# A hybrid decoder layer on one core: score maxima kept by group and reduced once per unit, reciprocals taken for two units at once

## The chip, the cores and the metric

The kernel runs on one core of a Trainium2 chip. The metric is the device time of one execution in microseconds, as the median of several runs. Times inside an execution come from one profiled execution, whose own time is given beside its span (from its first instruction to its last).

The core has engines that run side by side, each with its own queue of instructions in order: PE (matrix products, into PSUM), DVE (vector operations), ACT (activation functions, copies with a scale), POOL (a second, slower vector engine) and SP (which here issues transfers). They wait for each other through semaphores.

## The reference

The layer has forgetting attention with 8 heads of width 64 beside a gated short convolution, then an output projection and a convolutional feed-forward part, over 2048 positions of width 1024, all in float32. The change touches the attention alone:

```python
for i in range(s // BLOCK_Q):                    # 16 blocks of 128 queries
    q0, q1 = i * BLOCK_Q, (i + 1) * BLOCK_Q
    logits = einsum('bqhd,bkhd->bhqk', q[:, q0:q1], k[:, :q1]) * scale
    logits = logits + fcum[:, :, q0:q1, None] - fcum[:, :, None, :q1]
    logits = where(causal, logits, -inf)
    p = softmax(logits, axis=-1)
    outs.append(einsum('bhqk,bkhd->bqhd', p, v[:, :q1]))
```

A query block i sees (i + 1) blocks of 128 keys, and its softmax needs the row's maximum over all of them.

## The kernel before

The program has three stretches: projections and convolution (0 to 597 us of the span), attention (597 to 925 us), output projection and feed-forward part (925 us to the end).

In attention a **unit** is a pair of query blocks of one head, 15 - u and u for u = 0 to 7, so that each unit has 17 key blocks. There are 8 x 8 = 64 units, numbered n = 8h + u in what follows. The loop over s starts one unit per step, and each step runs five generators in turn, a piece of each per round: `weights` of unit s-1, `scores` of unit s, `divide_early` of unit s-4, `turn` of unit s-2 and `values` of unit s-4. Nearly all instructions are held in the order in which the program issues them, so this interleaving is each engine's queue.

What a unit goes through:

- `scores`: each query block's keys are cut into chunks of 512 columns, together five chunks per unit, taken in the order block 15-u, block u, block 15-u, and so on. PE makes a chunk's scores in a PSUM tile `ps` (lines 1053, 1054, and 1056 for the causal mask; four such tiles). DVE then adds the forget term `nf`, writes the scores to `s_t` and takes the running maximum into a column of `mx` (line 1077). This is one instruction with a second one behind it that reads the accumulator out. The operation of a block's later chunks starts its maximum from the column of the chunk before, through a pointer, so the last column holds the block's maximum. For u = 0 to 3 the first block has four chunks and the second one, so three chunks of the same block come one right after the other; for u = 4 to 7 the blocks alternate.
- `weights`: ACT scales the two maxima into a bias `nb` (line 1091) and runs two exponentials over `s_t` (line 1094), which also add up the row sums `l`.
- `turn`: POOL splits the far part of the weights into two halves (lines 1105, 1106), which a transfer transposes. For the near part PE transposes nine blocks into three PSUM tiles `pt` (line 1114), ACT evicts each to `near` (line 1116), and DVE subtracts for the low half (line 1121). DVE also takes the reciprocal of `l` here (line 1124).
- `values`: PE multiplies the weights with the values into `po` (lines 1150 to 1152). DVE divides, that is multiplies by the reciprocal (line 1165), and PE's next products into `po` wait for that.

Every second head, around u = 0 and u = 4, `store` transposes finished output and copies it out through ACT (`tm`, line 1184). In some steps ACT also takes sums over the output weights (`junk`, line 916).

Of the kernel before, what the change touches and what calls it, by code (L numbers as in the profile page):

```python
# [9 lines left out]
F32 = mybir.dt.float32  # L10
# [5 lines left out]
ALU = mybir.AluOpType  # L16
AX = mybir.AxisListType
# [3 lines left out]
P = 128  # L21
# [7 lines left out]
NT = S // P  # L29
# [17 lines left out]
def kernel(  # L47
# [20 lines left out]
    V, A, G, T = nc.vector, nc.scalar, nc.gpsimd, nc.tensor  # L68
# [72 lines left out]
    K = tc.keep_in_program_order  # L141
# [872 lines left out]
    with ExitStack() as ph:  # L1014
        cs = ph.enter_context(tc.tile_pool(name="cs", bufs=6))
# [28 lines left out]
        def product(g):  # L1044

            if len(products) > g:
                return
            while len(products) < min(g + GROUP, len(chunks)):
                h, u, _, i, c0, cw, last = chunks[len(products)]
                kh, qs, kl, nf = heads[h]  # L1050
                qt = qs[:, i * P : (i + 1) * P]
                ps = ps_s.tile([P, 512], F32, tag="s", name="ps")
                K(T.matmul(ps[:, 0:cw], lhsT=qt, rhs=kh[:, c0 : c0 + cw], start=True, stop=False))  # L1053
                K(T.matmul(ps[:, 0:cw], lhsT=qt, rhs=kl[:, c0 : c0 + cw], start=False, stop=not last))  # L1054
                if last:
                    K(T.matmul(ps[:, cw - P : cw], lhsT=ident_b, rhs=maskb, start=False, stop=True))  # L1056
                products.append(ps)

        taken[0] = 0

        def scores(un):

            nf = heads[un["h"]][3]
            un["s"] = s_t = cs.tile([P, WU], F32, tag="s", name="s_t", bufs=3)
            mx = cs.tile([P, 4, 4], F32, tag="mx", name="mx")[:, 0:2, :]
            un["l"] = cs.tile([P, 2], F32, tag="l", name="l", bufs=12)
            un["parts"] = [(NT - 1 - un["u"], NT - un["u"], 0), (un["u"], un["u"] + 1, NT - un["u"])]
            ends = [0, 0]
            while taken[0] < len(chunks) and chunks[taken[0]][:2] == (un["h"], un["u"]):
                _, _, p, i, c0, cw, last = chunks[taken[0]]  # L1070
                o0 = p * (NT - un["u"]) * P
                product(taken[0] + LEAD)
                ps = products[taken[0]]
                products[taken[0]] = None
                taken[0] += 1
                g = c0 // 512
                K(V.tensor_tensor_reduce(  # L1077
                    out=s_t[:, o0 + c0 : o0 + c0 + cw], in0=ps[:, 0:cw], in1=nf[:, c0 : c0 + cw], scale=1.0,
                    scalar=-3.0e38 if g == 0 else mx[:, p, g - 1 : g],
                    op0=ALU.add, op1=ALU.max, accum_out=mx[:, p, g : g + 1],  # L1080
                ))
                if last:
                    ends[p] = 4 * p + g
                yield
            un["mx"] = mx.rearrange("p a g -> p (a g)")[:, ends[0] : ends[1] + 1 : ends[1] - ends[0]]

        def weights(un):

# [9 lines left out]
        def turn(un):  # L1098

            s_t = un["s"]  # L1100
            near = cp.tile([P, 2, WB, P], F16, tag="near", name="near", bufs=3)
            far = cp.tile([P, 2, NT + 1 - WB, P], F16, tag="far", name="far", bufs=3)
            un["t"] = near, far
            wide = un["wide"]
            K(G.tensor_scalar(wide[:, 0, :], s_t[:, WB * P : WU], 1.0, 0.0, op0=ALU.mult, op1=ALU.add))
            K(G.tensor_tensor(wide[:, 1, :], s_t[:, WB * P : WU], wide[:, 0, :], op=ALU.subtract))  # L1106
            nc.sync.dma_start_transpose(far.rearrange("p a b n -> p (a b) n"), wide.rearrange("p a n -> p (a n)"))
            late = []

            def blocks(b0):  # L1110
                nb = min(4, WB - b0)
                pt = ps_x.tile([P, 512], F32, tag="x", name="pt")
                for b in range(nb):
                    K(T.transpose(pt[:, b * P : (b + 1) * P], s_t[:, (b0 + b) * P : (b0 + b + 1) * P], ident))  # L1114
                th, tl = [near[:, a, b0 : b0 + nb, :].rearrange("p b n -> p (b n)") for a in range(2)]
                K(A.activation(th, pt[:, 0 : nb * P], AF.Copy))  # L1116
                late.append((tl, pt[:, 0 : nb * P], th))

            def rest():
                tl, pt, th = late.pop(0)  # L1120
                K(V.tensor_tensor(tl, pt, th, op=ALU.subtract))  # L1121

            yield
            K(V.reciprocal(un["l"], un["l"]))
            yield
            blocks(0)
            yield
            blocks(4)
            yield
            blocks(8)  # L1130
            rest()
            yield
            rest()
            yield
            rest()
# [52 lines left out]
        units = []  # L1188
# [4 lines left out]
        for s in range(H * nu + 8):  # L1193
            h, u = divmod(s, nu)
# [13 lines left out]
            for back, stage in ((1, weights), (0, scores), (4, divide_early), (2, turn), (4, values)):  # L1208
                if 0 <= s - back < H * nu:
                    run.append(stage(units[s - back]))  # L1210
# [39 lines left out]
    with ExitStack() as ph:  # L1250
# [104 lines left out]
        def norm2_late(Q):  # L1355
# [19 lines left out]
            if Q % 2 == 0:  # L1375
                for k in range(4):
                    for n, name in enumerate(("b11", "b21")):
                        affine = turn(Q, 4 * n + k)
                        if later:
                            later.pop()()  # L1380
                        yield
                        h = affine()
                        hi, lo = pair(name, k)
                        high(h, hi)
                        later.append(lambda h=h, hi=hi, lo=lo: low(h, hi, lo))
                        yield
                later.pop()()
                yield
                return
# [38 lines left out]
            for k in range(4):  # L1428
                first = turn(Q, k)
                go_on()  # L1430
                yield
                b1 = first()
                go_on()
                yield
                second = turn(Q, 4 + k)
                go_on()
                yield
                b2 = second()
                go_on()
                running.append(sums(k, b1, b2))  # L1440
                yield
# [393 lines left out]
```

## Time and profile before

| | us |
|---|---|
| median of 3 runs | 2356.49 |
| lowest and highest run | 2356.17, 2357.16 |
| profiled execution, its own time | 2353.64 |
| its span | 2351.9 |
| mean granted clock of PE | 0.997 |
| PE busy over the span | 2270.3 |
| DVE busy over the span | 1742.2 |
| ACT busy over the span | 1164.3 |
| POOL busy over the span | 339.2 |

In a row of the profile, "L1077 DVE ... s_t<-ps,nf,mx" is line, engine, operation, and the tiles written and read. The group rows give shape, count, busy time in us, mean ns of one, and idle time of the engine ahead of them. Instructions overlap a little: the next may start before the one ahead has ended, so a pace is read from start to start. In rows by time the first number is the start, the second the duration, and square brackets hold the idle time ahead and what ended it.

### The profile page before, as it was taken

To read this page: it belongs to the slowest core of one execution; us is meant where nothing else is said; L and a number is where in the kernel's file an instruction comes from. 1 tells how busy PE (TensorE), PEld (TensorE's weight loads), DVE (VectorE), ACT (ScalarE), POOL (GpSimd) and SP (SyncE) were. 2 spreads that over 40 slices of the span, in tenths; PEclk is the share of its full clock that TensorE was granted. 3 is DMA by queue.
4 is the path that set the end of the run, shared out by engine and by line. 5 is a ranking of instruction groups with operands and counts; after the bars stand their busy time and mean duration, and the time that the engine had idled before them with its cause. 6 is when DMAs were issued, how large, how long until landed. Compare 5 with 4: busy or idle time off the path is not lost.

```text
span 2351.9 us, 38578 instructions
## 1 busy us (share of the span) xinstructions
PE 2270.3 (97%) x14208; PEld 1354.2 (58%) x14208; DVE 1742.2 (74%) x3414; ACT 1164.3 (50%) x1992; POOL 339.2 (14%) x282
## 2 busy tenths in 40 slices
PE   5899999999899998999999999999999999999999
PEld 5765554444577776444444444588764444446887
DVE  6768895773899998556899999966966565656556
ACT  5745453321688887343555565565522223224333
POOL 0211111111688874001000000000000000000000
PEclk9999999999999999999999999999999999999999
DMA  9346599973799986534456656577764454445766
GB/s 287 136 151 183 157 263 291 301 238 90 150 195 191 215 170 138 190 108 163 155 192 224 217 199 210 213 264 236 219 224 147 153 161 143 156 158 190 234 210 220
DMA packets 452646, 455.25 MB, mean 194 GB/s; under 512 B 191248, under 2 KB 301160, under 8 KB 451432
## 3 DMA queue, kind: packets, MB, share of 16 engines
q1 hardware_dynamic: 445336, 435.94, 62.4%
q10 hardware_dynamic: 4752, 8.46, 1.0%
q0 software_dynamic: 2368, 8.39, 0.9%
q8 instruction: 111, 1.82, 0.3%
q14 instruction: 79, 0.65, 0.1%
HBM read 284.84 MB, written 134.28 MB: 178 GB/s over the span
## 4 chain that ended last, share of the span: by engine, by line
PE 80%; DVE 11%; ACT 5%; issue 2%; DMA 1%; SPq 1%; POOL 0%; DVEq 0%; ACTq 0%
PE acc L1611 28%; PE acc L1788 16%; PE acc L145 13%; PE pr L145 11%; PE pv L145 2%; DVE s_t L1077 2%; PE pt L1114 2%; DVE near L1121 2%; PE ps L1053 1%; ACT s_t L1094 1%; PE ps L1054 1%; DVE t L1446 1%; PE po L1150 1%; ACT near L1116 1%; PE po L1152 1%
## 5 line engine op out<-in xcount | busy, mean ns | idle before, releaser
L1611 PEld LDWEIGHTS <-pair 128*128 128x128 f16 x3696 | 361.5, 98 | 439.7 <-issue 5.0
L1611 PE MATMUL acc<-t,pair 128*128 128x512 f16 x2112 | 477.4, 379 | 1.9 <-DVE t L1446 1.9
L1611 PE MATMUL acc<-b,pair 128*128 128x512 f16 x1584 | 363.4, 379 | 0.0
L1624 DVE SCALAR_TENSOR_TENSOR w<-w,fcw,w 128x1024 f32<-128x1024 f32 x176 | 226.1, 1285 | 79.4 <-ACT w L1619 73.2
L1535 DVE TENSOR_TENSOR lo<-raw,hi 128x1024 fp32r<-128x1024 f32 x154 | 187.4, 1223 | 115.8 <-ACT hi L1534 106.6
L1534 ACT ACTIVATE hi<-raw 128x1024 fp32r<-128x1024 f32 x154 | 161.1, 1057 | 172.6 <-PE acc L1788 117.9
L1788 PE MATMUL acc<-lo,hi 128*128 128x512 f32 x616 | 240.3, 390 | 2.9 <-DVE lo L1535 2.7
L1788 PE MATMUL acc<-hi 128*128 128x512 f32 x616 | 241.9, 393 | 0.0
L1788 PE MATMUL acc<-hi,lo 128*128 128x512 f32 x616 | 240.1, 390 | 0.0
L145 PEld LDWEIGHTS <-h 128*128 128x128 f16 x1344 | 130.3, 98 | 97.5 <-DVE h L358 5.4
L1619 ACT ACTIVATE w<-w,fcw 128x1024 f32<-128x1024 f32 x88 | 100.6, 1144 | 160.7 <-DVE w L1446 160.7
L145 PE MATMUL acc<-wp,mp 128*128 128x512 f16 x756 | 168.8, 382 | 2.8 <-ACT mp L954 1.4
L1094 ACT ACTIVATE s_t<-s_t,nb,cst 128x2048 f32<-128x2048 f32 (+15 forms) x128 | 164.7, 1288 | 5.8
L1106 POOL TENSOR_TENSOR wide<-s_t,wide 128x1024 f16<-128x1024 f32 x64 | 136.8, 2137 | 5.3
L1077 DVE CUSTOM_DVE_ANT_0 s_t<-ps,nf,mx 128x512 f32<-128x512 f32 (+1 forms) x192 | 119.4, 643 | 17.1 <-PE ps L1056 9.2
L1788 PEld LDWEIGHTS acc<-lo,hi 128*128 128x128 f32 x616 | 115.7, 188 | 28.1 <-DVE lo L1535 4.7
L1788 PEld LDWEIGHTS acc<-hi 128*128 128x128 f32 x616 | 115.7, 188 | 24.3 <-ACT hi L1534 0.4
L1788 PEld LDWEIGHTS acc<-hi,lo 128*128 128x128 f32 x616 | 115.6, 188 | 24.3
L145 PE MATMUL pr<-h,wh 128*128 128x512 f16 x576 | 126.5, 379 | 0.0
L145 PEld LDWEIGHTS <-mp 128*128 128x128 f16 x756 | 74.0, 98 | 90.1 <-issue 3.6
L145 PE MATMUL pr<-h,wl 128*128 128x512 f16 x576 | 125.8, 379 | 0.0
L1053 PE MATMUL ps<-kh,qs 128*128 128x512 f16 (+1 forms) x320 | 110.2, 348 | 13.2 <-DVE mx L1077 11.3
(369 smaller groups left out, 4091.1 us busy)
## 6 DMA issues: line engine op xcount, KB each, us to landing
up_sc<-pair SPq DMA_DIRECT2D x132, 256.0 KB, 2.7
pair<-up_sc SPq DMA_DIRECT2D x132, 256.0 KB, 3.0
wx<-in_w_up_dram SPq DMA_DIRECT2D x88, 256.0 KB, 3.7
raw<-in_w_up_dram SPq DMA_DIRECT2D x44, 512.0 KB, 3.7
y_t<-t SPq DMA_DIRECT2D x88, 256.0 KB, 2.7
raw<-y_t SPq DMA_DIRECT2D x88, 256.0 KB, 3.4
raw<-w_sc SPq DMA_DIRECT2D x88, 256.0 KB, 4.7
y_b<-y SPq DMA_DIRECT2D x66, 256.0 KB, 2.0
```

The costliest lines, as they stand in the source:

```text
L145: ins = T.matmul(acc, lhsT=a, rhs=b, start=st, stop=sp)
L1053: K(T.matmul(ps[:, 0:cw], lhsT=qt, rhs=kh[:, c0 : c0 + cw], start=True, stop=False))
L1077: K(V.tensor_tensor_reduce(out=s_t[:, o0 + c0 : o0 + c0 + cw], in0=ps[:, 0:cw], in1=nf[:, c0 : c0 + cw], scale=1.0, scalar=-3.0e38 if g == ...
L1094: K(A.activation(cols, cols, AF.Exp, bias=nb[:, p : p + 1], scale=qk[:, 4:5], accum_out=un["l"][:, p : p + 1]))
L1106: K(G.tensor_tensor(wide[:, 1, :], s_t[:, WB * P : WU], wide[:, 0, :], op=ALU.subtract))
L1114: K(T.transpose(pt[:, b * P : (b + 1) * P], s_t[:, (b0 + b) * P : (b0 + b + 1) * P], ident))
L1534: K(A.activation(hi, raw, AF.Copy))
L1535: K(V.tensor_tensor(lo, raw, hi.bitcast(F32), op=ALU.subtract))
L1611: K(T.matmul(acc, lhsT=a, rhs=b, start=st, stop=sp, skip_group_check=True))
L1619: K(A.activation(y, u[:, 0:1024], AF.Copy, scale=fcw[:, ct : ct + 1]))
L1624: K(V.scalar_tensor_tensor(y, u[:, m : m + 1024], fcw[:, m * 44 + ct : m * 44 + ct + 1], y, op0=ALU.mult, op1=ALU.add))
L1788: K(T.matmul(acc[t], lhsT=a[:, c], rhs=b, start=st, stop=sp, skip_group_check=True))
```

## The change

Three edits, all in the attention stretch:

- Each chunk's maximum is taken by itself, from the constant -3.0e38, into column g of its block in a tile `top` of 2 x 4 columns. There are eight such tiles, one for each u, which stay for all heads; POOL sets them to -3.0e38 once, before attention. A column that a unit doesn't use keeps that value.
- After a unit's five chunks one DVE `tensor_reduce` takes the maximum over the four columns of both blocks into a small `mx`, from which ACT makes `nb`. The generator issues it one round later than the last chunk.
- The row sums of two units share one tile of four columns, and one reciprocal of the four is taken in `turn` of the odd unit.

```diff
+        tops = [cs.tile([P, 2, 4], F32, name=f"top{u}", bufs=1) for u in range(NT // 2)]
+        for top in tops:
+            G.memset(top, -3.0e38)
...
-            mx = cs.tile([P, 4, 4], F32, tag="mx", name="mx")[:, 0:2, :]
-            un["l"] = cs.tile([P, 2], F32, tag="l", name="l", bufs=12)
+            mx = tops[un["u"]]
+            if un["u"] % 2 == 0:
+                un["ll"] = cs.tile([P, 4], F32, tag="l", name="l", bufs=6)
+            else:
+                un["ll"] = units[-2]["ll"]
+            un["l"] = un["ll"][:, 2 * (un["u"] % 2) : 2 * (un["u"] % 2) + 2]
...
-                    scalar=-3.0e38 if g == 0 else mx[:, p, g - 1 : g],
+                    scalar=-3.0e38,
...
-                if last:
-                    ends[p] = 4 * p + g
                 yield
-            un["mx"] = mx.rearrange("p a g -> p (a g)")[:, ends[0] : ends[1] + 1 : ends[1] - ends[0]]
+            un["mx"] = cs.tile([P, 2], F32, tag="mx", name="mx")
+            K(V.tensor_reduce(un["mx"], mx, axis=AX.X, op=ALU.max))
...
-            K(V.reciprocal(un["l"], un["l"]))
+            if un["u"] % 2:
+                K(V.reciprocal(un["ll"], un["ll"]))
```

The queues of PE, ACT and SP keep their order; POOL's gets the eight memsets. DVE's changes in each unit. Here is DVE's queue before for unit 24 (u = 0), from its first score operation to the subtractions of unit 22 that are issued in the same step. ISA is the score operation or, with `mx 128x1`, its read-out; the brackets name the engines and transfers it waits for.

```order
L1077 ISA s_t,mx<-ps,nf 128x512 [waits DMAHW4_49,PE_49,Pool_49]
L1077 ISA mx 128x1
L1077 ISA s_t,mx<-ps,nf 128x128 [waits PE_49]
L1077 ISA mx 128x1
L1124 RECIPROCAL l<-l 128x2
L1077 ISA s_t,mx<-ps,nf,mx 128x512 [waits DVE_49,PE_49]
L1077 ISA mx 128x1
...
L1121 TENSOR_TENSOR near<-pt,near 128x512 [waits Activation_49] x2
L1165 TENSOR_TENSOR at<-po,l 128x2x64 [waits PE_49]
L1121 TENSOR_TENSOR near<-pt,near 128x128 [waits Activation_49]
```

(The fourth and fifth score operations, left out, read like the third.) And DVE's queue with the change at the same place, where `top_6769` is the persistent tile of u = 0:

```order
L1083 ISA s_t,top_6769<-ps,nf 128x512 [waits DMAHW4_49,PE_49,Pool_49]
L1083 ISA top_6769 128x1
L1083 ISA s_t,top_6769<-ps,nf 128x128 [waits PE_49]
L1083 ISA top_6769 128x1
L1083 ISA s_t,top_6769<-ps,nf 128x512 [waits PE_49]
L1083 ISA top_6769 128x1
...
L1126 TENSOR_TENSOR near<-pt,near 128x512 [waits Activation_49]
L1090 TENSOR_REDUCE mx<-top_6769 128x2 [waits DVE_49]
L1126 TENSOR_TENSOR near<-pt,near 128x512 [waits Activation_49]
L1171 TENSOR_TENSOR at<-po,l 128x2x64 [waits PE_49]
L1126 TENSOR_TENSOR near<-pt,near 128x128 [waits Activation_49]
```

(Here too the fourth and the fifth are left out.) The waits of score operations on DVE itself are gone, the reciprocal has left this even unit, and a reduction stands between the first and the second subtraction.

The second place is unit 29 (u = 5), DVE's queue from its last score operation to the first of unit 30, before:

```order
L1077 ISA s_t,mx<-ps,nf,mx 128x384 [waits DVE_49,PE_49]
L1077 ISA mx 128x1
L1121 TENSOR_TENSOR near<-pt,near 128x512 [waits Activation_49]
L1165 TENSOR_TENSOR at<-po,l 128x2x64 [waits PE_49]
L1121 TENSOR_TENSOR near<-pt,near 128x512 [waits Activation_49]
L1121 TENSOR_TENSOR near<-pt,near 128x128 [waits Activation_49]
L1077 ISA s_t,mx<-ps,nf 128x512 [waits PE_49,Pool_49]
```

and with the change (`top_6774` and `top_6775` are the tiles of u = 5 and u = 6):

```order
L1083 ISA s_t,top_6774<-ps,nf 128x384 [waits PE_49]
L1083 ISA top_6774 128x1
L1126 TENSOR_TENSOR near<-pt,near 128x512 [waits Activation_49]
L1171 TENSOR_TENSOR at<-po,l 128x2x64 [waits PE_49]
L1090 TENSOR_REDUCE mx<-top_6774 128x2 [waits DVE_49]
L1126 TENSOR_TENSOR near<-pt,near 128x512 [waits Activation_49]
L1126 TENSOR_TENSOR near<-pt,near 128x128 [waits Activation_49]
L1083 ISA s_t,top_6775<-ps,nf 128x512 [waits PE_49,Pool_49]
```

The reduction, and with it what ACT needs for `nb`, now stands behind the first subtraction and the divide; before, ACT needed the last score operation alone.

More of the change, by code (lines that the diff above doesn't have):

```diff
@@ L1064, in scores @@
             un["s"] = s_t = cs.tile([P, WU], F32, tag="s", name="s_t", bufs=3)
-            mx = cs.tile([P, 4, 4], F32, tag="mx", name="mx")[:, 0:2, :]
-            un["l"] = cs.tile([P, 2], F32, tag="l", name="l", bufs=12)
+            mx = tops[un["u"]]
[4 more added lines that the diff above has]
+            un["l"] = un["ll"][:, 2 * (un["u"] % 2) : 2 * (un["u"] % 2) + 2]
             un["parts"] = [(NT - 1 - un["u"], NT - un["u"], 0), (un["u"], un["u"] + 1, NT - un["u"])]
-            ends = [0, 0]
             while taken[0] < len(chunks) and chunks[taken[0]][:2] == (un["h"], un["u"]):
```

## The prediction

> **What bounds the kernel now.** I read the busy time by stretch first, then who waited for whom inside the attention stretch, then the instructions of one head in order of time. The change touches the attention stretch alone, 597 to 925 us of the span. The first fence has its row of the busy table, then rows of the waits inside it (total us, times, longest).
>
> ```profile
> core 0: us, PE busy (x) PEld busy (x) DVE busy (x) ACT busy (x) POOL busy (x), PEclk, DMA share, GB/s
> 597.00:925.00 328.00, 298.46 (x4493) 231.28 (x4493) 300.24 (x965) 281.28 (x555) 248.26 (x158) 0.99 0.93 182
> ...
> ACT near L1116 <- PE pt L1114: 33.7, 53, 1.8
> ...
> PE po L1150 <- DVE at L1165: 14.9, 23, 2.1
> PE ps L1053 <- DVE mx L1077: 11.3, 15, 1.1
> DVE s_t L1077 <- PE ps L1056: 9.2, 15, 1.2
> DVE near L1121 <- ACT near L1116: 8.2, 15, 1.2
> ACT nb L1091 <- DVE mx L1077: 6.7, 4, 5.8
> ```
>
> DVE and PE are both about 91% busy (300.24 and 298.46 of 328 us), ACT 86%. No engine bounds the stretch alone: PE waits 14.9 + 11.3 = 26.2 us, all of it for DVE, and DVE waits 9.2 us for PE and 8.2 us for ACT. Those 26.2 us are the ceiling of what a faster DVE can give, since PE has the rest of the stretch to work through whatever DVE does. ACT waits little for the maxima (6.7 us, of which 5.8 are its first wait, while the stage starts) and much for PE's transposes (33.7 us). I number the units n = 8h + u. The next fence is DVE in order of time (start, us): two score operations of unit 31, then all five of unit 32.
>
> ```profile
> 750.14 0.73 DVE L1077 CUSTOM_DVE_ANT_0 s_t<-ps,nf,mx 128x512 f32<-128x512 f32 x1
> ...
> 750.80 0.75 DVE L1077 CUSTOM_DVE_ANT_0 s_t<-ps,nf,mx 128x512 f32<-128x512 f32 x1
> ...
> 754.19 0.68 DVE L1077 CUSTOM_DVE_ANT_0 s_t<-ps,nf 128x512 f32<-128x512 f32 x1
> 754.80 0.08 DVE L1077 DVE_READ_ACCUMULATOR2_ANT mx<- 128x1 f32 x1
> 754.80 0.28 DVE L1077 CUSTOM_DVE_ANT_0 s_t<-ps,nf 128x128 f32<-128x128 f32 x1
> ...
> 755.01 0.16 DVE L1124 RECIPROCAL l<-l 128x2 f32<-128x2 f32 x1
> 755.09 0.73 DVE L1077 CUSTOM_DVE_ANT_0 s_t<-ps,nf,mx 128x512 f32<-128x512 f32 x1
> 755.75 0.08 DVE L1077 DVE_READ_ACCUMULATOR2_ANT mx<- 128x1 f32 x1
> 755.97 0.75 DVE L1077 CUSTOM_DVE_ANT_0 s_t<-ps,nf,mx 128x512 f32<-128x512 f32 x1
> 756.65 0.08 DVE L1077 DVE_READ_ACCUMULATOR2_ANT mx<- 128x1 f32 x1
> 756.88 0.75 DVE L1077 CUSTOM_DVE_ANT_0 s_t<-ps,nf,mx 128x512 f32<-128x512 f32 x1
> 757.55 0.69 DVE L1121 TENSOR_TENSOR near<-pt,near 128x512 f16<-128x512 f32 x1
> ```
>
> Three paces stand there, from start to start of a 128x512 score operation. With a constant start value the next follows after 0.61 us (754.19 to 754.80). With a pointer to mx it takes 0.66 (750.14 to 750.80), where that maximum was read out well before. Where the maximum is the one that the operation just ahead has made, 0.88 and 0.91 (755.09, 755.97, 756.88): the accumulator is read out in 0.08, and DVE then stands still for 0.14.
>
> **The change, part by part.** *Score operations.* All 320 now take a constant. 192 lose the pointer, at 0.05 to 0.06 us each (0.66 to 0.61, and the two first rows below: 739 against 683 ns; I take the narrower forms as alike): 10.6 us. In units with u = 0 to 3 two more steps lose 0.88 to 0.91 for 0.61, of which 0.25 is beyond the pointer: 32 units x 2 x 0.25 = 16 us.
>
> ```profile
> L1077 DVE CUSTOM_DVE_ANT_0 s_t<-ps,nf,mx 128x512 f32<-128x512 f32 x120 | 88.2, 739 | 5.4
> ...
> L1077 DVE CUSTOM_DVE_ANT_0 s_t<-ps,nf 128x512 f32<-128x512 f32 x104 | 68.0, 683 | 0.0
> ...
> L1124 DVE RECIPROCAL l<-l 128x2 f32<-128x2 f32 x64 | 10.2, 160 | 0.0
> ...
> L921 DVE TENSOR_REDUCE rim<-vmax 128x1 f32<-128x16 f32 x1 | 0.2, 165 | 0.0
> ```
>
> *Reciprocals.* One takes 160 ns, but the next instruction starts 0.08 later (755.01 to 755.09). 32 go: 2.5 us. The 32 that stay are twice as wide, which I cost at nothing. *Reductions.* 64 come. The nearest row is L921, of twice the width, in this stretch and with POOL at work: 165 ns. Between 0.08 (it overlaps its successor as the reciprocal does) and 0.165 (no overlap) I take 0.08, the pace of the nearest instruction of that size: 5.1 us, at most 10.6. *Net on DVE's queue:* 10.6 + 16 + 2.5 - 5.1 = 24 us less. *Memsets.* Eight tiny ones on POOL, before the first score operation at 597.22; POOL idles 12.29 us there, so I cost them at nothing; without that cover the first units would start later by what they take.
>
> ```profile
> 603.87 1.05 POOL L1105 TENSOR_SCALAR wide<-s_t 128x1024 f16<-128x1024 f32 x1 [12.29 <-ACT s_t L1094]
> ```
>
> *The wait that comes.* In DVE's new order the reduction isn't behind the last score operation: it is behind the first `near` subtraction, which waits for ACT's eviction, and in most units behind the divide too, which waits for PE. Behind the reduction stand DVE's other subtractions; on ACT the instruction that waits for it, nb, has both exponentials and the next evictions behind it. So a ring is closed: eviction, `near`, divide, reduction, nb, exponentials, eviction. Rows of ACT and DVE at units 29 and 31:
>
> ```profile
> 742.15 1.22 ACT L1116 ACTIVATE near<-pt 128x512 f16<-128x512 f32 x3
> 743.27 0.29 ACT L1091 ACTIVATE nb<-mx,cst 128x2 f32<-128x2 f32 x1
> ...
> 748.25 0.28 ACT L1116 ACTIVATE near<-pt 128x128 f16<-128x128 f32 x1 [0.81 <-PE pt L1114]
> ...
> 742.76 0.69 DVE L1121 TENSOR_TENSOR near<-pt,near 128x512 f16<-128x512 f32 x1 [0.48 <-ACT near L1116]
> 743.37 0.28 DVE L1165 TENSOR_TENSOR at<-po,l 128x128 f32<-128x128 f32 x1
> 743.56 0.88 DVE L1121 TENSOR_TENSOR near<-pt,near 128x512 f16<-128x512 f32 x2
> ...
> 753.10 0.29 ACT L1091 ACTIVATE nb<-mx,cst 128x2 f32<-128x2 f32 x1
> ...
> 756.06 0.60 ACT L1116 ACTIVATE near<-pt 128x512 f16<-128x512 f32 x1
> 756.88 0.69 ACT L1184 ACTIVATE tm<-pt,vi 128x512 f32<-128x512 f32 x1 [0.22 <-DMA kh<-k_hi]
> 757.47 0.59 ACT L1116 ACTIVATE near<-pt 128x512 f16<-128x512 f32 x1
> ```
>
> At u = 5 the reduction can start at 743.56, end at 743.72, and nb follow at about 743.77 instead of 743.27: ACT loses 0.5 us. ACT's next wait, 0.81 for PE at 748.25, absorbs that. At u = 7 (753.10) it loses 0.5 again; there the evictions and the copy at 756.88 follow with gaps of 0.22 and little more. In the other units nb has its slack from DVE being earlier.
>
> *What reaches PE.* Here are PE's three longest waits of a head (718.96, 735.14, and 759.09 at the place of the first one, a head later), with the divide of unit 27 and PE's last product ahead of it:
>
> ```profile
> 718.96 0.19 PE L1150 MATMUL po<-v,near 128*128 128x64 f16 x1 [0.98 <-DVE at L1165]
> ...
> 732.07 0.19 PE L1152 MATMUL po<-v,far 128*128 128x64 f16 x1
> ...
> 735.14 0.38 PE L1053 MATMUL ps<-kh,qs 128*128 128x512 f16 x1 [0.97 <-DVE mx L1077]
> ...
> 732.80 0.29 DVE L1165 TENSOR_TENSOR at<-po,l 128x128 f32<-128x128 f32 x1
> ...
> 759.09 0.19 PE L1150 MATMUL po<-v,near 128*128 128x64 f16 x1 [0.54 <-DVE at L1165]
> ```
>
> From 718.96 to 735.14 PE has no wait of note, so DVE can run ahead only as far as its divides allow: that of unit 27 starts at 732.80, 0.54 after its last product (732.07 + 0.19). DVE could save 2 x (2 x 0.25 + 3 x 0.055) = 1.3 in units 26 and 27, but gains 0.54 less one reduction: 0.45 of the 0.97. Seven such heads: **-3.1**. The divide at u = 0 comes earlier by up to 0.35 in the three heads without a store there, and later by 0.2 in the three with one (the ring of unit 31, then the copy at 756.88): **-0.45**. At u = 4 a reduction stands ahead of the divide that PE waits for: 7 x 0.08 = **+0.6**. In the ramp, units 0 to 3, nothing else is in the way; DVE saves 2.7 there and pays for reductions that wait for the operation just ahead (2 x 0.33) and for nb; I take about half of the rest: **-1.0**. Sum: -4.0 us, an estimate. The profiled execution took 2353.64 us, its span 2351.9; so 2349.6 by it, and by the median of the runs (2356.49) **2352.5**.
>
> *A rule weighed.* The pace of 0.88 against 0.66 says that a wait for the operation just ahead costs 0.22 us. The Trainium skill ("VectorE: DVE Perf Modes", "The DRAIN you can't avoid") says otherwise: eight copies took the same time with a semaphore after each as with one at the end, so the wait would cost nothing extra. By that rule the 0.22 would stay, and it gives the second rival below; this trace doesn't bear it out where the wait is for an accumulator's read-out.
>
> **The rivals.** *DVE's gain reaches PE almost whole.* For it: from unit 26 to unit 28 DVE waits for no other engine. Against it: the divide's 0.54. If half of PE's 26.2 us goes, -8 to -16, so 2344. *The removed waits come back as something else* (the rule above: the read-out itself, not the wait, is what holds the next operation). Then only pointers and reciprocals are saved, 10.6 + 2.5 - 5.1 = 8 us on DVE, about a third of 24, so a third of the gains and all of the +0.6: about -1, 2355.5. For it: each score operation keeps its read-out. Against it: 754.80, where the next operation starts together with the read-out. *Slower: the ring.* nb is late by 0.5 us at u = 5 and u = 7, 16 times in the stretch: 8 us. It decides as soon as ACT's waits for PE behind it (0.81 and less) are shorter than 0.5, which is what an earlier PE brings about. Then DVE's `near` waits longer (8.2 us now), and +5 to +8 remains: 2363. Against it: 33.7 us of ACT's waits for PE.
>
> **How the numbers follow.** Forecast, a gain of 0 to 8 us around 4: 0.50. Nearly whole: 0.22. Waits that come back: 0.14. The ring: 0.14. A change of 0.2% is 4.7 us, about what a measurement of this kernel can tell from no change; 0.20 of the forecast's 0.50 lies beyond it. So faster 0.42, same 0.30 + 0.14 = 0.44, slower 0.14. The range leaves out the ring and the far end of the whole gain: 2343.5 to 2359, which also holds reductions at 0.165 (about +2 us).
>
> **What would show it.** Score operations at 0.61 from start to start, without 0.14 between; 64 reductions near 0.16 us, followed after 0.08; DVE busy in the stretch down by 8 to 12 us. PE's waits of 0.97 at u = 4 down to about 0.5. nb at u = 5 about 1.0 us behind the first eviction's end, and ACT's wait of 0.81 shorter by that. Wrong would be: score operations still at 0.88, PE's waits for DVE under 18 us or over 27, or ACT's waits for reductions over 10 us in sum.

## The result, and the profile after

| | before | change |
|---|---|---|
| median (runs) | 2355.89 us (13) | 2353.81 us (13) |
| lowest to highest | 2353.54 to 2360.79 | 2349.18 to 2356.58 |
| profiled execution, its own time (span) | 2353.64 (2351.9) | 2354.73 (2353.0) |

The ratio of change to before is 0.9983 (95% interval 0.9975 to 0.9992): 4 us faster, between 2 and 6; the medians are 2.1 us apart. A part of that is the clock: at a mean granted clock of 0.999, 0.998 and 0.997 the runs of before whose clock is on record average 2354.5, 2354.6 and 2357.6 us, and those of the change and its repeat e5 2351.8, 2353.0 and 2355.7, so 1.6 to 2.6 less at an equal clock.

To see the attention alone I compare a **stage** in the two profiled executions: from the start of the first score operation to the end of the last product of the output projection (`acc<-wp,mp`), which needs attention's last results. In the change these two rows stand at its ends (start, us):

```profile
599.49 0.69 DVE L1083 CUSTOM_DVE_ANT_0 s_t<-ps,nf 128x512 f32<-128x512 f32 x1
...
1113.30 1.03 PE L145 MATMUL acc<-wp,mp 128*128 128x512 f16 x4
```

1113.30 + 1.03 - 599.49 gives 514.8 us. The same rows of before start at 597.22 and end at 1114.66: 517.4. The stage is 2.6 us shorter.

But the clock of PE is not the same in the two. In before the granted clock falls to 0.5 for about 3.4 us at two places of the stage, in the change at none. Here are these two places, first in before, then in the change (the third number from the end is the clock):

```profile
885.00:889.00 4.00, 4.00 (x44) 3.13 (x43) 2.98 (x11) 1.62 (x5) 2.81 (x2) 0.57 0.81 162
1066.00:1070.00 4.00, 4.00 (x12) 1.47 (x11) 3.69 (x7) 2.15 (x4) 0.03 (x1) 0.57 0.36 126
...
885.00:889.00 4.00, 2.09 (x27) 1.37 (x26) 4.00 (x16) 2.46 (x4) 2.14 (x2) 1.00 0.70 152
1066.00:1070.00 4.00, 3.83 (x20) 2.05 (x21) 3.81 (x7) 3.37 (x6) 0.00 (x0) 1.00 0.44 131
```

Compared divide by divide with e6 below, which has the full clock there, before loses 1.2 us at the first place and 1.7 at the second. Without them its stage is 514.5 us (an estimate from these two steps), and the change's 514.8 is not shorter. The 1.6 to 2.6 us that the runs gain are not seen in this one execution of the change, whose own time, 2354.73, lies above the median. The change and its repeat e5 are the same program and have none and one such place, so such a place belongs to the execution at least in part; whether a kernel makes them rarer is not shown.

The busy row of the change for the same 328 us as in the prediction, then the groups by form of DVE:

```profile
597.00:925.00 328.00, 298.56 (x4497) 230.83 (x4497) 290.60 (x1006) 279.24 (x554) 247.42 (x165) 1.00 0.93 182
...
L1083 DVE CUSTOM_DVE_ANT_0 s_t<-ps,nf 128x512 f32<-128x512 f32 x224 | 144.8, 679 | 0.1
...
L1090 DVE TENSOR_REDUCE mx<-top 128x2 f32<-128x8 f32 x64 | 9.6, 150 | 0.1
```

DVE is busy 9.6 us less (300.24 to 290.60). All 224 wide score operations are now of the cheap kind, 679 ns, and the 64 reductions take 150 ns each. In order of time, DVE of the change from unit 29's first `near` subtraction on, then three score operations of unit 32 (u = 0), all of the same block:

```profile
745.60 0.69 DVE L1126 TENSOR_TENSOR near<-pt,near 128x512 f16<-128x512 f32 x1 [0.54 <-ACT near L1121]
746.21 0.28 DVE L1171 TENSOR_TENSOR at<-po,l 128x128 f32<-128x128 f32 x1
746.41 0.15 DVE L1090 TENSOR_REDUCE mx<-top 128x2 f32<-128x8 f32 x1
746.47 0.88 DVE L1126 TENSOR_TENSOR near<-pt,near 128x512 f16<-128x512 f32 x2
...
757.98 0.68 DVE L1083 CUSTOM_DVE_ANT_0 s_t<-ps,nf 128x512 f32<-128x512 f32 x1
758.59 0.08 DVE L1083 DVE_READ_ACCUMULATOR2_ANT top<- 128x1 f32 x1
758.59 0.69 DVE L1083 CUSTOM_DVE_ANT_0 s_t<-ps,nf 128x512 f32<-128x512 f32 x1
759.20 0.08 DVE L1083 DVE_READ_ACCUMULATOR2_ANT top<- 128x1 f32 x1
759.20 0.69 DVE L1083 CUSTOM_DVE_ANT_0 s_t<-ps,nf 128x512 f32<-128x512 f32 x1
```

Score operations of one block follow each other at 757.98, 758.59, 759.20: 0.61 us, where before took 0.88 to 0.91 at the same unit, and the next one starts together with the read-out ahead of it. The reduction (746.41) stands behind a subtraction that waited 0.54 for ACT, and behind the divide; the instruction after it starts 0.06 later. The waits of the same stage (total us, times, longest):

```profile
ACT near L1121 <- PE pt L1119: 29.6, 46, 1.4
...
DVE near L1126 <- ACT near L1121: 15.8, 38, 1.3
...
DVE s_t L1083 <- PE ps L1056: 12.5, 16, 1.3
...
PE po L1156 <- DVE at L1171: 12.3, 20, 1.9
ACT nb L1096 <- DVE mx L1090: 11.7, 17, 5.3
...
PE ps L1053 <- DVE top L1083: 9.3, 23, 1.2
...
PE po L1156 <- DMA far<-wide: 4.9, 7, 1.4
```

PE's waits for DVE are down from 26.2 to 21.6 us. The last row is **new**: PE waits 4.9 us for `far`, the transposed weights, on which it never waited before. As far as waits go, what PE gained on DVE it gives back to a transfer. Three of the seven places, in order of time:

```profile
655.86 0.20 PE L1156 MATMUL po<-v,far 128*128 128x64 f16 x1 [0.71 <-DMA far<-wide]
...
738.99 0.20 PE L1156 MATMUL po<-v,far 128*128 128x64 f16 x1 [1.41 <-DMA far<-wide]
...
816.13 0.20 PE L1156 MATMUL po<-v,far 128*128 128x64 f16 x1 [1.16 <-DMA far<-wide]
```

These are at units 8, 24 and 39; the others are at 16, 23, 32 and 40, around the change of a head.

### The profile page after: what moved, and what is told of

The parts are those of the page before. It is cut to its first block, busy times and chain, and to the rows that moved or that the text cites. A ratio compares the mean times of both kernels' runs of the same rounds, so it can differ in the third digit from the quotient of the medians.

```text
span 2353.0 us, 38435 instructions
## 1 busy us (share of the span) xinstructions
PE 2269.6 (96%) x14208; PEld 1354.6 (58%) x14208; DVE 1730.1 (74%) x3446; ACT 1163.5 (49%) x1992; POOL 339.9 (14%) x290
## 4 chain that ended last, share of the span: by engine, by line
PE 76%; DVE 10%; ACT 5%; DMA 5%; issue 2%; SPq 1%; POOL 1%; ACTq 0%; DVEq 0%; POOLq 0%
PE acc L1617 28%; PE acc L1794 14%; PE acc L145 13%; PE pr L145 11%; DMA far<-wide 2%; PE pv L145 2%; ACT s_t L1099 2%; PE pt L1119 1%; PE ps L1053 1%; PE ps L1054 1%; DVE near L1126 1%; DVE t L1452 1%; DVE lo L1541 1%; PE po L1156 1%; ACT near L1121 1%
## 5 line engine op out<-in xcount | busy, mean ns | idle before, releaser
L1083 DVE CUSTOM_DVE_ANT_0 s_t<-ps,nf 128x512 f32<-128x512 f32 (+1 forms) x320 | 177.4, 601 | 12.5 <-PE ps L1056 12.5
```

The costliest lines, as they stand in the source:

```text
L1083: K(V.tensor_tensor_reduce(out=s_t[:, o0 + c0 : o0 + c0 + cw], in0=ps[:, 0:cw], in1=nf[:, c0 : c0 + cw], scale=1.0, scalar=-3.0e38, op0=AL ...
```

## The experiments

All in one table; "stage" is measured as above in each profiled execution, "half clock" counts its places with the clock at 0.5, "full clock" is an estimate of the stage without them, and "landing" is the shortest time from issue to landing of a transposing transfer in the stage.

| kernel | ratio to before | median us (runs) | stage us | half clock | full clock us | PE waits for DVE, us | PE waits for `far`, us | landing us |
|---|---|---|---|---|---|---|---|---|
| before | 1 | 2355.89 (13) | 517.44 | 2 | 514.5 | 26.2 | 0 | 4.2 |
| change | 0.9983 | 2353.81 (13) | 514.83 | 0 | 514.8 | 21.6 | 4.9 | 4.3 |
| e1 reciprocals alone | 0.9989 (0.998 to 0.9999) | 2353.42 (11) | 517.20 | 2 | 514.3 | 26.5 | 0 | 3.6 |
| e2 maxima alone | 0.9977 (0.9967 to 0.9987) | 2349.89 (8) | 509.09 | 0 | 509.1 | 21.5 | 0.2 | 3.6 |
| e9 maxima alone again | 0.9968 (0.9957 to 0.998) | 2349.14 (11) | 510.90 | 1 | 510.0 | 21.4 | 0.7 | 3.6 |
| e5 change again | 0.9993 (0.9981 to 1.0005) | 2354.44 (11) | 515.66 | 1 | 514.0 to 515.7 | 20.9 | 4.8 | 4.3 |
| e3 reduction at once | 0.9989 (0.998 to 0.9998) | 2353.33 (11) | 511.65 | 1 | 509.9 to 511.7 | 20.7 | 1.9 | 4.3 |
| e4 at once, u = 5 and 7 | 0.9989 (0.998 to 0.9999) | 2353.35 (11) | 514.86 | 0 | 514.9 | 19.3 | 6.0 | 4.3 |
| e6 before, seven loads less | 1.0001 (0.9992 to 1.001) | 2354.42 (11) | 515.38 | 1 | 514.5 | 26.2 | 0 | 4.2 |
| e7 change, seven loads less | 0.9973 (0.9962 to 0.9985) | 2348.82 (6) | 508.78 | 0 | 508.8 | 21.4 | 0 | 4.3 |
| e8 maxima, seven loads less | 0.997 (0.9958 to 0.9981) | 2347.47 (6) | 508.78 | 0 | 508.8 | 21.4 | 0 | 3.7 |
| e10 loads from ACT | 1.0028 (1.0007 to 1.005) | 2365.74 (12) | 514.76 | 1 | 513.9 | 21.8 | 2.5 | 4.2 |
| e11 loads in halves | 0.9986 (0.9975 to 0.9998) | 2353.59 (11) | 516.47 | 3 | 512.3 | 21.6 | 2.7 | 4.3 |
| e12 reductions twice | 0.9999 (0.9988 to 1.001) | 2356.33 (11) | 515.93 | 0 | 515.9 | 26.9 | 1.3 | 4.2 |

The runs of before that e1 to e4 are compared with had a median of 2356.04, those of e5 to e8 2355.13, those of e9 to e12 2355.14. What the half clock cost is read from the step that it makes against a kernel with the full clock there: 0.9 to 1.7 us a place. In e3 and e5 it falls together with a wait for `far`, so there the two bounds are nothing and 1.7 us, half of 3.4.

### The two halves of the change: e1 and e2

e1 is the kernel before with the paired reciprocals only:

```diff
-            un["l"] = cs.tile([P, 2], F32, tag="l", name="l", bufs=12)
+            if un["u"] % 2 == 0:
+                un["ll"] = cs.tile([P, 4], F32, tag="l", name="l", bufs=6)
...
-            K(V.reciprocal(un["l"], un["l"]))
+            if un["u"] % 2:
+                K(V.reciprocal(un["ll"], un["ll"]))
```

> Only the reciprocals are paired, the maxima stay as before. Theory A (the gain is DVE time saved at the score operations): 32 x 0.08 us of DVE go, of which at most a third reaches PE, so about -0.5 us, a ratio of 0.9998, not to be told from 1. Rival B (the reciprocals carry a good part): -2 us or more, 0.9990 or less.

The stage is 0.24 us shorter, with the half clock at the same two places as before, and PE's waits for DVE are the same. The ratio, 0.9989, lies on the side of rival B, but its interval reaches almost to 1, and its runs had a higher mean clock (0.9983) than those of before beside them (0.9974). By the stage, the pairing by itself gives next to nothing.

e2 is the change with one reciprocal per unit, as before:

```diff
-            if un["u"] % 2 == 0:
-                un["ll"] = cs.tile([P, 4], F32, tag="l", name="l", bufs=6)
...
+            un["l"] = cs.tile([P, 2], F32, tag="l", name="l", bufs=12)
...
-            if un["u"] % 2:
-                K(V.reciprocal(un["ll"], un["ll"]))
+            K(V.reciprocal(un["l"], un["l"]))
```

> Only the maxima are changed, each unit keeps its own reciprocal. Theory A: nearly the whole gain, -3 to -4 us, ratio 0.9984 to 0.9988, and PE's waits of 0.97 us at u = 4 shrink to about 0.57 as with both. Rival B: near 1.

The maxima alone gain more than the whole change, and more than was expected: 8.35 us of the stage, of which 2.9 are the half clock of before, so 5.4. Its ends and its two waits:

```profile
598.72 0.69 DVE L1079 CUSTOM_DVE_ANT_0 s_t<-ps,nf 128x512 f32<-128x512 f32 x1
...
1103.76 4.05 PE L145 MATMUL acc<-wp,mp 128*128 128x512 f16 x18
...
PE po L1151 <- DVE at L1166: 12.5, 20, 1.9
...
PE ps L1053 <- DVE top L1079: 9.0, 21, 1.2
...
PE po L1151 <- DMA far<-wide: 0.2, 1, 0.2
```

PE waits for DVE as long as in the change (21.5 against 21.6), so DVE's side is not the difference. The wait for `far` is: 0.2 against 4.9. I had no theory for that, and the next runs look for one.

### The ring through nb: e3 and e4

Both issue the reduction directly behind the last score operation, ahead of the subtraction that waits for ACT; e3 in all units, e4 (with `un["u"] in (5, 7)` in place of `True`) where nb was late:

```diff
                 ))
+                if True and not (taken[0] < len(chunks) and chunks[taken[0]][:2] == (un["h"], un["u"])):
+                    break
                 yield
```

> As the change, but each reduction stands directly behind the unit's last score operation. ACT's waits for reductions (11.7 us in 17 times with the change) then shrink to about 6, and DVE stands still about 0.25 us ahead of each reduction wherever it isn't idle anyway. Theory A (the late nb is absorbed by ACT's waits for PE): no gain, -2 to -4 us against before, 0.9983 to 0.9992. Rival C (the ring through nb costs 3 us or more): 0.9970 or less.

> As the change, but in units with u = 5 and u = 7, where DVE idles 0.5 to 1.0 us ahead of its first subtraction, the reduction stands directly behind the last score operation, so that it costs DVE nothing. Theory A: 0 to 1 us better than the change, -4 to -5 us, 0.9979 to 0.9983. Rival C (the ring costs): 3 us or more better, -7 us or more, 0.9970 or less.

ACT's wait for the reduction all but disappears in e3:

```profile
ACT nb L1098 <- DVE mx L1092: 5.7, 2, 5.3
...
PE po L1158 <- DMA far<-wide: 1.9, 2, 1.5
```

5.3 of the 5.7 is its first wait, while the stage starts; in the change it is 11.7, of which 5.3. So the ring cost ACT 6 us. At unit 20, ahead of most waits for `far`, e3's divide stands 0.23 us earlier than that of e7 below, which has the ring and no wait for `far` (118.61 against 118.84 us from the stage's start); e3 had waited 0.42 for `far` by then. The ring is worth 0.2 to 0.7 us up to there, and neither e3 nor e4 is faster than the change beyond the interval; e4 misses the small gain that was expected of it (0.9979 to 0.9983), with 6.0 us of waits for `far`. (That e3's stage is shorter than the change's goes with its 1.9 us of such waits in place of 4.9.) That agrees with the prediction: ACT's waits for PE absorb it.

### The transfers: e5 to e8

e5 is the change once more. e6, e7 and e8 are before, the change and the maxima alone with seven transfers of 1 MB left out: the forget row `nf` of head 0 is used in all heads.

```diff
-            t = sp.tile([P, S], F32, tag="nf", name="nf")
-            load(t, nf_sc[h].partition_broadcast(P))
+            if h == 0:
+                t = sp.tile([P, S], F32, tag="nf", name="nf", bufs=1)
+                load(t, nf_sc[h].partition_broadcast(P))
+            else:
+                t = heads[0][3]
+                steps.append(lambda: None)
```

> The change itself, unaltered, to see whether what PE waited for the transposing transfers (4.9 us in 7 times) belongs to the change or to the run. From the first score operation to the last product of the output projection it took 514.8 us against 517.4 before, and 509.1 with the maxima alone. Theory D (transfers that land late, at places that differ from run to run): PE's waits for them differ from 4.9 by more than 1 us, and the stretch with them. Rival E (the paired reciprocals bring them about): again 4 to 6 us at the same units, stretch 514 to 516 us. Ratio 0.998 to 0.999 by both.

> The kernel before with the forget row of head 0 used for all heads: seven loads of 1 MB each are left out (and with them the forget terms of heads 1 to 7), so that the transfers have room. Theory D: PE waits for no transfer before and none here, so nearly nothing, 0 to -1 us, ratio 0.9996 to 1. If transfers hold PE in another way that the waits don't show: -2 us or more.

> The change with the same seven loads (and forget terms) left out. Theory D: PE's waits for the transposing transfers go, the stretch from the first score operation to the last product of the output projection becomes 508 to 510 us, ratio to before 0.9965 to 0.9975, so that the change gains 7 us beside its own before (e6). Rival E (the paired reciprocals): waits of 4 to 6 us stay, ratio 0.998 or more.

> The maxima alone with the same seven loads left out. Theory D: as e7 within 1 us, stretch 508 to 510 us. Rival E: 4 to 6 us shorter than e7.

The change repeats: 4.8 us of waits for `far`, at units 16, 19, 24, 32, 39 and 40. Without the seven loads they are gone, and the stage is 508.78 us with and without the pairing. The ends of e7 (the row between is left out) and its waits:

```profile
597.79 0.69 DVE L1087 CUSTOM_DVE_ANT_0 s_t<-ps,nf 128x512 f32<-128x512 f32 x1
...
1103.81 2.75 PE L145 MATMUL acc<-wp,mp 128*128 128x512 f16 x12
...
PE po L1160 <- DVE at L1175: 12.5, 20, 1.9
...
PE ps L1057 <- DVE top L1087: 8.9, 20, 1.2
```

Compared divide by divide, the distance between the change and e7 is steady to 0.02 us from unit 9 to 15, from 17 to 22, from 25 to 31, from 33 to 38 and from 41 to the end; it grows around units 8, 16, 23, 24, 32, 39 and 40 alone, the seven places where the change waits for `far`, to 6.06 us. That the given-back 6 us are late transfers is therefore shown: take away bytes that share their way, and exactly these steps go. In the kernel before the loads cost nothing: before and e6 keep step to 0.04 us up to unit 52, the whole program is at 1.0001, and the 2.06 us between the stages come from places where one of the two has the half clock. That of e6 stands here:

```profile
925.00:929.00 4.00, 4.00 (x15) 1.46 (x12) 3.04 (x6) 2.29 (x5) 1.94 (x1) 0.57 0.53 132
```

So the maxima's gain with the transfers out of the way is e7 against e6, 6.6 us, less the 0.9 that e6 loses at 925 us: 5.7 us.

### Why the maxima alone escape: e9, e10, e11

e9 is e2 once more. e10 issues the 1 MB loads from ACT, e11 splits each in two halves one unit apart:

```diff
-            load(t, nf_sc[h].partition_broadcast(P))
+            steps.append(lambda: nc.scalar.dma_start(t, nf_sc[h].partition_broadcast(P)))
```

```diff
-            load(t, nf_sc[h].partition_broadcast(P))
...
+            half = lambda c: nc.sync.dma_start(t[:, c : c + S // 2], nf_sc[h : h + 1, c : c + S // 2].partition_broadcast(P))
...
+            steps.append(lambda: half(0))
+            steps.append(lambda: (half(S // 2), copy(ks[0])))
...
```

> The change with one reciprocal per unit, a second time (the maxima alone). In its first run it had a stretch of 509.09 us and 0.2 us of PE's waits for transposing transfers, where the whole change had 514.83 and 515.66, with 4.9 and 4.8 us. Theory E1 (the pairing of the reciprocals, by when it lets the divides and the store go, makes the transfers late): this run again has under 1 us of those waits and a stretch of 508.5 to 510.5 us; ratio 0.997 to 0.998. Theory E2 (chance of that run: small shifts decide which transposing transfers meet the others): 2 to 6 us of those waits and a stretch of 511 to 516; ratio 0.998 to 0.9995.

> The change, with the 1 MB loads of the forget row issued by ScalarE instead of SyncE; the same bytes move. If the late transposing transfers come from standing behind those loads in SyncE's queue: PE's waits for them fall from 4.9 to under 1 us and the stretch from 515 to 508.5 to 510.5 us, ratio 0.997 to 0.998. If they come from sharing the 16 transfer engines, by whichever queue: the waits stay at 3 to 7 us and the stretch at 513 to 517, ratio 0.998 to 0.9995. [...]

> The change, with each 1 MB load of the forget row as two halves of 0.5 MB, one unit apart, both from SyncE; the same bytes move. If one long load ahead of a transposing transfer is what makes it late: PE's waits for these fall from 4.9 to under 2 us, the stretch from 515 to 508.5 to 512 us, ratio 0.997 to 0.9985. If the sum of the bytes in the stretch does it: waits of 3 to 7 us and a stretch of 513 to 517, ratio 0.998 to 0.9995.

e9 has 0.7 us of waits for `far` and the best ratio of all full kernels, 0.9968; its stage, 510.90, lies 0.4 above what was expected, but 0.9 of it is a place with the half clock. With e2 that is two of two without the pairing, against 4.9 and 4.8 with it. So together with the maxima the pairing does cost 4 to 6 us of the stage (an estimate from the full-clock column), though by itself it costs nothing (e1) and nothing where the loads are gone (e7 and e8). It cannot be its work on DVE, whose times agree to 0.02 us between the waits.

What does differ shows in the view of `far`'s own instructions. The change, the kernel before, the maxima alone and the reciprocals alone, in this order, by SP's issues (count, ns shortest, median, longest) and the times to landing:

```profile
L1112 SPq DMA_TRANSPOSE far<-wide x63: 1777/3056/7311, 609.0 to 923.0; - x63
...
DMA to landing us min/median/max: 4.3/4.8/10.4
```

```profile
L1107 SPq DMA_TRANSPOSE far<-wide x63: 1670/3008/6700, 607.2 to 921.6; - x63
...
DMA to landing us min/median/max: 4.2/4.8/9.5
```

```profile
L1108 SPq DMA_TRANSPOSE far<-wide x64: 1580/2260/7703, 608.2 to 921.7; - x64
...
DMA to landing us min/median/max: 3.6/4.4/9.9
```

```profile
L1111 SPq DMA_TRANSPOSE far<-wide x63: 1581/2028/7705, 610.4 to 924.7; - x63
...
DMA to landing us min/median/max: 3.6/4.0/9.0
```

The same transfer of the same bytes lands after 3.6 us at the least in the last two and after 4.2 or more in the first two. Over all fourteen kernels it is 3.6 or 3.7 in e1, e2, e8 and e9 and 4.2 or 4.3 in the ten others; it goes neither with the pairing (e1 has it, e2 not) nor with the maxima. It goes with **where the buffers lie**. Small tiles ahead of them in SBUF changed size and number, so that `wide` starts at byte 137472 of each partition in e1 and 137728 in e2, e8 and e9, both multiples of 256; in before and e6 at 137664 (192 beyond a multiple), in the change and the seven others at 137536 (64 beyond). `far` starts 26112 bytes, a multiple of 256, behind `wide` in all of them. So beside the maxima alone the change has transfers that are 0.6 us longer, and with PE ahead of its old pace I take it that no slack was left for them. The Trainium skill ("DMA: Bandwidth & Descriptors", "How a descriptor splits into AXI transactions") has a rule that fits: a transaction must start at a multiple of 256 bytes, so for a descriptor that starts elsewhere the bytes from the boundary below it are fetched too, unused, and still cost beats of 32 bytes. The trace agrees in the sign; the packets here are of 256 bytes (2048 of them with 0.52 MB in 2 us of e9). But moving these buffers and nothing else was not tried: that their place is the cause is read from fourteen kernels, not shown by a run of its own.

e10 and e11 tell less. The waits for `far` fall to 2.5 and 2.7 us, between what the two readings expected. Their stages look as long as the change's, but e10 has one place with the half clock and e11 three, more than any other; without these e10's is about 1 us shorter than the change's and e11's 2.5. In e10 ACT takes 326 ns for an issue where SP took 530, and DVE's waits for ACT's `near` are 22.8 us instead of 15.8. Its times fall in two groups: five of twelve runs at 2351.0 to 2355.4, the profiled one among them, seven at 2364.9 to 2377.2, with a mean clock of 0.998 to 0.999 in the five and 0.995 to 0.996 in the seven. What else the seven lose no profile shows; it stays open. Neither another queue nor shorter loads does away with the late transfers, though shorter loads take some of them away.

### The price of a reduction: e12

```diff
             K(V.tensor_reduce(un["mx"], mx, axis=AX.X, op=ALU.max))
+            K(V.tensor_reduce(un["mx"], mx, axis=AX.X, op=ALU.max))
```

> The change with each of the 64 reductions issued twice. At the prediction's price of 0.08 us each, DVE gets 5.1 us more; of the prediction's +0.6 (u = 4) and ramp share, about 1 us more reaches the end: stretch 515.5 to 517, ratio 0.9985 to 0.9998. Rival: each reduction is paid in full on PE's path (0.08 to 0.16 us, 64 times): stretch 520 to 526, ratio 1.0005 to 1.003. The groups by form should show 128 reductions of 0.15 us, and a start to start of 0.07 to 0.08 us from the first to the second if they overlap, 0.15 if the second waits.

DVE of e12 at one of the units:

```profile
755.17 0.28 DVE L1172 TENSOR_TENSOR at<-po,l 128x128 f32<-128x128 f32 x1
755.37 0.15 DVE L1090 TENSOR_REDUCE mx<-top 128x2 f32<-128x8 f32 x1
755.55 0.16 DVE L1091 TENSOR_REDUCE mx<-top 128x2 f32<-128x8 f32 x1
755.63 0.88 DVE L1127 TENSOR_TENSOR near<-pt,near 128x512 f16<-128x512 f32 x2
```

The second one writes what the first writes, and starts 0.18 us behind it, more than either expectation; an instruction that waits for neither starts 0.08 behind the second. So 64 x 0.18 = 11.5 us went on DVE's queue, and PE's waits for DVE grew from 21.6 to 26.9. Against e7, which has no waits for `far`, the stage is 7.15 us longer, 1.3 of it such waits: roughly half of what is put on DVE's queue reaches the end (an estimate). The stage came out as the first reading expected, by luck: the reductions cost about 5.9 us of it and not 1, and 3.6 us of the change's waits for `far` went. The ratio is a hair above that reading's upper end.

## Why the prediction was right, and where it wasn't

It forecast 2352.5 us, 4.0 less; measured were 2353.81 and a ratio of 4 us less. The mechanism on DVE was right, but the agreement of the sum is luck: with the transfers out of the way DVE's gain was 5.7 us and not 4.0, late transfers that the prediction had at nothing took back 6 in the profiled stage, and at an equal clock 1.6 to 2.6 us of the 4 are left.

- **Score operations.** Forecast 0.61 us from start to start with nothing between; the rows at 757.98 show it. The rival by which the waits come back fell with that, and so did the rule of the Trainium skill ("VectorE: DVE Perf Modes", "The DRAIN you can't avoid") for this case: with the wait on the operation just ahead removed, the pace fell from 0.88 to 0.61, of which the pointer is 0.05.
- **Reductions.** 150 ns and 0.06 to 0.08 to the next instruction where nothing waits, as forecast.
- **DVE busy.** 8 to 12 us less forecast, 9.6 measured. **Memsets.** Nothing: the first score operation starts 442.7 us behind the first `acc` product of the program in the change, and 442.6 in before.
- **Reciprocals.** Costed at -2.5 us on DVE's queue; e1 gives 0.24 us of the stage for all of it.
- **Units.** The divide that the prediction calls that of unit 27 (732.80) belongs to unit 23 and is issued in the step of unit 27; its sum doesn't change by that.
- **PE at u = 4.** Forecast 0.97 to about 0.5, measured 0.57:

```profile
736.40 0.38 PE L1053 MATMUL ps<-kh,qs 128*128 128x512 f16 x1 [0.57 <-DVE top L1083]
```

- **The ring.** nb at u = 5 about 1.0 us behind the first eviction's end, and ACT's 0.81 shorter. ACT of the change at unit 29:

```profile
744.99 1.23 ACT L1121 ACTIVATE near<-pt 128x512 f16<-128x512 f32 x3
746.59 0.29 ACT L1096 ACTIVATE nb<-mx,cst 128x2 f32<-128x2 f32 x1 [0.37 <-DVE mx L1090]
...
751.15 0.28 ACT L1121 ACTIVATE near<-pt 128x128 f16<-128x128 f32 x1 [0.54 <-PE pt L1119]
```

  The three evictions end at 746.22, the first at about 745.6; nb is 1.0 behind it, and the wait is 0.54. ACT's waits for reductions came to 11.7 us, over the 10 that I had called a sign of being wrong. That bound was badly chosen: it holds the first wait of 5.3, and e3 shows that the rest costs less than 1 us.
- **The sum.** Its terms can be read from e7 against e6, where transfers are out of the way. Ramp, to the divide of unit 4: -1.5 (forecast -1.0). From there to unit 48, five and a half heads: -2.8, or 0.51 a head (forecast 0.42). From unit 48 to the end: -2.3, of which 0.9 is e6's half clock, so -1.4 (forecast some -0.4). The last head was under-sized most; in before PE waits 0.95, 0.31 and 2.08 us for the divides of units 50 to 52, in e7 0.82, none and 1.91, and its wait of 0.97 at u = 4 falls to 0.58. Together -5.7 for -4.0.
- **The term that was missing.** The prediction took it that PE has no other wait of note, and priced no transfer. The given-back 6 us, 4.9 of them as PE's waits for `far`, are what it lacked. Of the rivals, the one where DVE's gain reaches PE almost whole (-8 to -16) was not met even by the maxima alone: -5.4 us of the stage in e2 without the half clock of before.

The maxima alone (e2, e9) beat both kernels: 2349.89 and 2349.14 us, ratios 0.9977 and 0.9968; their runs also had a higher mean clock (0.9985, before 0.9975), and at 0.998 they average 2350.5 us.

## What to carry to other kernels

When an engine that waited for another is let run ahead, look next at what lands just in time: a transfer with no wait in the profile may have no slack either, and the wait that comes is on none of the engines that were costed. Split a change into its halves and time them, even where one half looks free: here the half that looked free, which also moved buffers by some bytes, took back more than half of what the other gave. Before two stages are compared, look at the granted clock inside each: two places of 3.4 us at half speed looked like a gain of 2.9. Here a maximum taken from a constant, with one reduction at the end, was cheaper than one that is carried through a pointer from the operation just ahead.

## What the runs showed of the hardware

- The same transposing transfer lands at the earliest after 3.6 us or 4.2, by kernel and not by run, and all four kernels with 3.6 have its buffers at multiples of 256 bytes.
- The granted clock of PE falls to 0.5 for about 3.4 us at a time, at different places in two executions of the same program, and each place cost the stage 0.9 to 1.7 us where it can be told apart.
- A carried maximum costs twice: the pointer some 0.05 us, and the wait for the read-out just ahead 0.22 to 0.25.
- Between two waits for transfers, two kernels that differ in one small DVE instruction per unit keep step to 0.02 us over 100 us and more; differences in such a stage come in steps, and the steps say where.
